# Convolution of the delta projections read from an SBUF copy with zero columns between the streams

## The chip, the cores and the metric

One core of a Trainium2 chip runs the whole program as one launch. The metric is the device time in microseconds (us) from its start to its end; the lower, the better. TensorE (PE) multiplies matrices into PSUM, VectorE (DVE), ScalarE (ACT) and GpSimd (POOL) work element by element, and SyncE (SP) issues most DMAs. Each engine runs its own instructions in the order in which they were queued, and waits on semaphores for the others.

## The reference

Two layers of a diffusion trunk over 256 context and 512 latent tokens of width 1024, in float32. Layer 0 mixes tokens by a gated delta rule, layer 1 by retention; each is followed by a squared-ReLU MLP. The change lies in layer 0, in the part between the projection and the recurrence:

```python
def short_conv(x, w):            # w: 4 taps for each channel, padding (2, 1)
    return lax.conv_general_dilated(x, w[:, None, :].astype(x.dtype), window_strides=(1,),
                                    padding=[CONV_PAD], dimension_numbers=('NWC', 'WIO', 'NWC'),
                                    feature_group_count=x.shape[-1])

def gdn_mixer(hc, hl, w_in, conv_w, ...):
    n_ctx = hc.shape[1]                                       # 256
    proj = jnp.concatenate([hc, hl], axis=1) @ w_in           # 768 tokens
    qkv = proj[..., :GDN_CONV_DIM]                            # 4096 channels: q 1024, k 1024, v 2048
    z = proj[..., GDN_CONV_DIM:GDN_CONV_DIM + GDN_VALUE_DIM]  # 2048 channels, no convolution
    qkv = jnp.concatenate([jax.nn.silu(short_conv(qkv[:, :n_ctx], conv_w)),
                           jax.nn.silu(short_conv(qkv[:, n_ctx:], conv_w))], axis=1)
    ...                          # l2norm of q and k, then chunks of 64 tokens, in both directions
```

The two streams, context and latent, are convolved apart: each begins and ends with zeros, and no tap reaches from one into the other.

## The kernel before, in words

Tokens lie on the free axis and channels on the 128 partitions. The projection is made in tiles of 128 channels: 32 convolution tiles (8 of q, 8 of k, 16 of v) and 16 z tiles. For one tile, w_cols loads the weights in two halves and splits each into a high and a low part (hl, one ACT and one DVE operation each; lines 55 to 57), and gemm_pair makes 24 matmuls of 512 latent columns into a PSUM tile gl and 24 of 256 context columns into gc. In this layer `self.gc = ("gl", 2)`, so gl and gc take turns in one ring of two PSUM slots: the gl of the next tile takes the slot of this tile's gl.

conv_tile then makes the four taps. ACT copies a segment from PSUM to acc, scaled by tap 2, and DVE adds taps 0, 1 and 3, each read from PSUM with its offset: three operations for gl (510 or 511 columns) and three for gc (254 or 255). The Silu of acc goes to kq (gdn_s1, k and q) or vt (gdn_sv, v). acc has two buffers in the pool prep, shared with sq, the squares for the norm, and with zs, the Silu of a z tile on its way to DRAM (z_tile).

Two heads make a pair, and there are eight. gdn_s1 and gdn_sv prepare the pair's k, q and v; gdn_bt makes decay factors e, 24 blocks of 128 columns first by a Relu (line 649), then by an Exp (657); gdn_s2 makes qkd and the triangular blocks, and eliminates in u (a select on POOL at 709, then 30 steps of two short DVE operations, 717 and 720); gdn_iv puts the inverse together (tt) through v32, xdg, pc and pc2; gdn_step runs twelve recurrence steps, each a chain from PE (kk, uo) through DVE (r, s) and ACT (und, un) back to PE; gdn_y normalises. layer0_mix issues the work of the next pairs between the steps of the present one, with priorities (PRI, P2, PS) for the steps and their preparation; convolution and z tiles fill the rest. A list scheduler turns this into the order of each queue, by the priorities and by when it takes operands and buffers to be ready; the order is fixed when the program is built. mod_rows (line 232) is further filling work. After the layer follow out0, the first MLP, the retention layer and the second MLP, which the change does not touch.

Of the kernel before, what the change touches and what calls it, by code (L numbers as in the profile page):

```python
# [10 lines left out]
F32 = mybir.dt.float32  # L11
BF16 = mybir.dt.bfloat16
F32R = mybir.dt.float32r
AF = mybir.ActivationFunctionType
ALU = mybir.AluOpType
# [4 lines left out]
NC_T = 256  # L20
NL_T = 512
T = NC_T + NL_T
# [3 lines left out]
NCH = 6  # L26
CH = 128
# [15 lines left out]
class Trunk:  # L43
# [393 lines left out]
    def z_tile(self, h, prep):  # L437
        nc = self.nc
        w = self.w_cols(self.i["gdn_w_in"][0][:, 4096 + h * 128:4096 + (h + 1) * 128])
        zs = prep.tile([128, T], F32, tag="acc", name="zs", bufs=2)  # L440
        for ps, t0, n in self.gemm_pair(w):
            nc.scalar.activation(out=zs[:, t0:t0 + n], in_=ps, func=AF.Silu)  # L442
        nc.sync.dma_start(out=self.zd[h], in_=zs)
# [128 lines left out]
    def conv_tile(self, prep, tile_i):  # L572
        nc = self.nc
        w = self.w_cols(self.i["gdn_w_in"][0][:, tile_i * 128:(tile_i + 1) * 128])
        c = [self.cw[:, j * 32 + tile_i:j * 32 + tile_i + 1] for j in range(4)]
        segs = self.gemm_pair(w)
        acc = prep.tile([128, T], F32, tag="acc", name="acc", bufs=2)
        for ps, t0, n in segs:
            nc.scalar.activation(out=acc[:, t0:t0 + n], in_=ps, func=AF.Copy, scale=c[2])  # L579
            for j, a, b in ((0, 2, 0), (1, 1, 0), (3, 0, 1)):  # L580
                m = n - max(a, b)
                nc.vector.scalar_tensor_tensor(  # L582
                    out=acc[:, t0 + a:t0 + a + m], in0=ps[:, b:b + m], scalar=c[j], in1=acc[:, t0 + a:t0 + a + m],
                    op0=ALU.mult, op1=ALU.add)
        return acc

    def gdn_s1(self, p, st, psk, scan, prep):
        nc = self.nc
        kq = scan.tile([128, NCH, 2 * CH], F32, tag="kq", name="kq", bufs=3)
        st["kq"] = kq  # L590
        acc = self.conv_tile(prep, 8 + p).rearrange("p (c i) -> p c i", i=CH)
        nc.scalar.activation(out=kq[:, :, 0:CH], in_=acc, func=AF.Silu)
        yield
        acc = self.conv_tile(prep, p).rearrange("p (c i) -> p c i", i=CH)
        nc.scalar.activation(out=kq[:, :, CH:2 * CH], in_=acc, func=AF.Silu)
        yield
        ps = psk.tile([128, 2, NCH], F32, tag="py", name="ssps")
        for hf in range(2):
            sq = prep.tile([128, 3, 2, CH], F32, tag="acc", name="sq", bufs=2)
            nc.scalar.activation(  # L600
                out=sq.rearrange("p c a i -> p c (a i)"), in_=kq[:, hf * 3:hf * 3 + 3], func=AF.Square)
            for c in range(3):
                for a in range(2):
                    nc.tensor.matmul(
                        ps[:, a, hf * 3 + c:hf * 3 + c + 1], lhsT=sq[:, c, a], rhs=self.ones[:, 0:1],
                        start=True, stop=True)
        ssk = prep.tile([128, NCH], F32, tag="ssk", name="ssk", bufs=2)
        sg = scan.tile([128, NCH], F32, tag="sg", name="sg", bufs=3)
        nc.vector.tensor_scalar_add(ssk, ps[:, 0], EPS)
        nc.vector.tensor_scalar(  # L610
            out=sg, in0=ps[:, 1], scalar1=128.0 * EPS, scalar2=EPS + 128.0 * EPS * EPS, op0=ALU.mult, op1=ALU.add)
        rk = prep.tile([128, NCH], F32, tag="rk", name="rk")
        self.rsq(rk, ssk)
        nk = scan.tile([128, NCH], F32, tag="nk", name="nk", bufs=3)
        nc.vector.scalar_tensor_tensor(out=nk, in0=ssk, scalar=-1.0, in1=rk, op0=ALU.mult, op1=ALU.mult)
        nc.gpsimd.tensor_tensor(out=rk, in0=rk, in1=rk, op=ALU.mult)
        we = scan.tile([128, 2, 2, NCH], F32, tag="we", name="we", bufs=3)
        for d in range(2):
            nc.gpsimd.tensor_tensor(
                out=we[:, d], in0=self.egl[:, d, 2 * p:2 * p + 2], in1=rk.unsqueeze(1).to_broadcast([128, 2, NCH]),  # L620
                op=ALU.mult)
        st.update(sg=sg, nk=nk, we=we, ssk=ssk)

    def gdn_sv(self, p, st, prep):
        vt = prep.tile([128, 2, T], F32, tag="vt", name="vt")
        st["vt"] = vt
        for h in range(2):
            acc = self.conv_tile(prep, 16 + 2 * p + h)
            self.nc.scalar.activation(out=vt[:, h], in_=acc, func=AF.Silu)
            yield  # L630

    def gdn_bt(self, p, st, prep):
# [92 lines left out]
    def gdn_iv(self, p, st, psk, prep, tags=("pp",), gate=None):  # L725
        nc = self.nc
        tts, vd, v64 = st["tts"], self.vd[p % 2], self.v64
        off32, off64 = st["off32"], st["off64"]
        N = 2 * NCH
        gsl = [slice(g * 32, (g + 1) * 32) for g in range(4)]  # L730
        half = [slice(0, 64), slice(64, 128)]
        with self.tc.issue_after(gate) if gate is not None else ExitStack():
            for d in range(2):
                nc.scalar.dma_start(
                    out=vd[d].rearrange("c g r q -> (c g) (r q)"), in_=self.u[d * 64:d * 64 + 48])
# [15 lines left out]
        ps = psk.tile([128, N, 32], F32, tag=next(tags), name="ivps")  # L751
# [14 lines left out]
        ps = psk.tile([128, N, 32], F32, tag=next(tags), name="ivps2")  # L766
# [8 lines left out]
            else:  # L775
                nc.vector.tensor_copy(dst, ps[gsl[ra]])
        yield
        pc2 = prep.tile([128, N, 64], F32, tag="pc2", name="pc2")
        for hf in range(2):
            cs = range(hf * NCH, (hf + 1) * NCH)  # L780
            ps = psk.tile([128, NCH, 64], F32, tag=next(tags), name="ivps4")
            for c in cs:
                for d in range(2):
                    nc.tensor.matmul(
                        ps[half[1 - d], c - hf * NCH], lhsT=off64[half[d], c], rhs=v64[half[d], c],
                        start=True, stop=True)
            if hf:
                nc.vector.tensor_copy(pc2[:, hf * NCH:(hf + 1) * NCH], ps)
            else:
                nc.scalar.activation(out=pc2[:, hf * NCH:(hf + 1) * NCH], in_=ps, func=AF.Copy)  # L790
        yield
        for hf in range(2):
            cs = range(hf * NCH, (hf + 1) * NCH)
            ps = psk.tile([128, NCH, 64], F32, tag=next(tags), name="ivps5")
            for c in cs:
                for d in range(2):
                    nc.tensor.matmul(
                        ps[half[d], c - hf * NCH], lhsT=pc2[half[1 - d], c], rhs=tts[d][half[1 - d], c, half[1 - d]],
                        start=True, stop=True)
            for d in range(2):  # L800
                dst = tts[d][half[d], hf * NCH:(hf + 1) * NCH, half[1 - d]]
                if d == 0:
                    nc.scalar.activation(out=dst, in_=ps[half[d]], func=AF.Copy)
                else:
                    nc.vector.tensor_copy(dst, ps[half[d]])
# [572 lines left out]
```

## Time and profile before

| | us |
|---|---|
| median of 3 runs | 2560.19 (2559.29 to 2561.56) |
| the profiled execution | 2564.44 |
| its span in the trace | 2562.7 |
| PE, DVE, ACT, POOL busy over the span | 2431.7, 1661.7, 1074.0, 163.7 |
| the stage of the convolutions, 60 to 890 us: PE, DVE, ACT, POOL busy | 735.59, 611.95, 486.93, 119.34 |

The profiled execution is a run of its own, 4.25 us above the median; durations and waits come from it alone. A row of the groups names the line, the engine and the operation, what it writes and reads, the shapes, the count, the busy time, the mean time of one in ns, and the idle time of the engine just before, with what ended it. A row of the waits says which engine and line waited for which, the total, how often, and the longest. A row in order of time has the start, the length, and in brackets the idle time ahead and its releaser. A row of the stretches has busy time and (instructions) of PE, weight loads, DVE, ACT and POOL, then the granted TensorE clock, the DMA share and GB/s.

### The profile page before, as it was taken

To read this page: it belongs to the slowest core of one execution; us is meant where nothing else is said; L and a number is where in the kernel's file an instruction comes from. 1 tells how busy PE (TensorE), PEld (TensorE's weight loads), DVE (VectorE), ACT (ScalarE), POOL (GpSimd) and SP (SyncE) were. 2 spreads that over 40 slices of the span, in tenths; PEclk is the share of its full clock that TensorE was granted. 3 is DMA by queue.
4 is the path that set the end of the run, shared out by engine and by line. 5 is a ranking of instruction groups with operands and counts; after the bars stand their busy time and mean duration, and the time that the engine had idled before them with its cause. 6 is when DMAs were issued, how large, how long until landed. Compare 5 with 4: busy or idle time off the path is not lost.

```text
span 2562.7 us, 38997 instructions
## 1 busy us (share of the span) xinstructions
PE 2431.7 (95%) x14879; PEld 2010.7 (78%) x14879; DVE 1661.7 (65%) x3382; ACT 1074.0 (42%) x2357; POOL 163.7 (6%) x248
## 2 busy tenths in 40 slices
PE   8799798998888999999999999999999999999998
PEld 4687686786777787878888888888888887788887
DVE  5568767777776845887876667874353546644446
ACT  5576556565654553253222222653231322532222
POOL 1101111111201110000000000000000000000000
PEclk9899899899999999999999999999999999999999
DMA  6332324333132238354444444243122223433332
GB/s 211 89 96 77 106 51 113 80 105 94 43 109 67 74 113 272 132 165 132 132 144 129 123 130 129 100 135 93 50 84 61 78 66 115 150 97 91 107 91 91
DMA packets 346828, 276.94 MB, mean 108 GB/s; under 512 B 105608, under 2 KB 293488, under 8 KB 346640
## 3 DMA queue, kind: packets, MB, share of 16 engines
q1 hardware_dynamic: 345616, 271.30, 35.2%
q10 hardware_dynamic: 1024, 3.15, 0.5%
q8 instruction: 117, 1.92, 0.3%
q14 instruction: 71, 0.58, 0.1%
HBM read 241.72 MB, written 32.67 MB: 107 GB/s over the span
## 4 chain that ended last, share of the span: by engine, by line
PE 58%; DVE 5%; DMA 2%; ACT 2%; issue 1%; POOL 0%; SPq 0%; POOLq 0%; DVEq 0%; ACTq 0%
PE pn L940 22%; PE gl L91 14%; PE rvp L1257 5%; PE gc L91 3%; PE rl L91 3%; PE rgp L1257 3%; PE pv L1287 3%; PE sc L1265 1%; PE rc L91 1%; PE nps L276 1%; DVE hl L57 0%; DVE ma L199 0%; DMA zt<-zd 0%; PE mps L214 0%; PE uo L865 0%
## 5 line engine op out<-in xcount | busy, mean ns | idle before, releaser
L91 PE MATMUL gl<-xt,hl 128*128 128x512 f32 (+2 forms) x2760 | 704.6, 404 | 53.9 <-DVE acc L582 31.9
L91 PEld LDWEIGHTS gl<-xt,hl 128*128 128x128 f32 x2760 | 517.0, 194 | 161.9 <-issue 27.9
L57 DVE TENSOR_TENSOR hl<-raw,hl 128x1024 fp32r<-128x1024 f32 (+1 forms) x306 | 321.4, 1052 | 231.1 <-ACT hl L56 230.3
L56 ACT ACTIVATE hl<-raw 128x1024 fp32r<-128x1024 f32 (+1 forms) x306 | 280.0, 920 | 409.6 <-PE pn L940 251.9
L940 PE MATMUL pn<-hl,fh 128*128 128x512 f32 x1920 | 444.7, 391 | 2.2 <-DVE fh L1074 1.9
L940 PEld LDWEIGHTS pn<-hl,fh 128*128 128x128 f32 x1920 | 357.3, 188 | 80.0 <-DVE fh L1074 5.0
L91 PE MATMUL gc<-xt,hl 128*128 128x256 f32 x1944 | 273.2, 289 | 8.9 <-DVE acc L582 4.7
L91 PEld LDWEIGHTS gc<-xt,hl 128*128 128x128 f32 x1944 | 253.3, 193 | 19.9 <-ACT zs L442 5.5
L199 DVE SCALAR_TENSOR_TENSOR ma<-mraw,cst,ma 128x256 f32<-128x256 f32 x280 | 123.5, 482 | 40.4 <-DMA mraw<-in_w_mod 38.1
L940 PE MATMUL pn<-hl,yh 128*128 128x512 f32 x576 | 133.8, 392 | 2.5 <-ACT yh L56 1.4
L954 DVE TENSOR_TENSOR facc<-pn,facc 128x512 f32<-128x512 f32 x120 | 82.5, 689 | 81.8 <-PE pn L940 81.5
L1257 PE MATMUL rvp<-hl,xt 128*128 128x512 f32 x576 | 132.8, 389 | 0.0
L940 PEld LDWEIGHTS pn<-hl,yh 128*128 128x128 f32 x576 | 107.2, 188 | 26.8 <-ACT yh L56 2.6
L1257 PEld LDWEIGHTS rvp<-hl,xt 128*128 128x128 f32 x576 | 107.8, 188 | 22.2
L1071 ACT ACTIVATE fr<-gl 128x512 f32<-128x512 f32 x64 | 38.2, 597 | 193.3 <-PE gl L91 190.7
L582 DVE SCALAR_TENSOR_TENSOR acc<-gl,cw,acc 128x511 f32<-128x511 f32 (+1 forms) x96 | 71.6, 746 | 37.9 <-ACT acc L579 37.1
L940 PE MATMUL pn<-hl,ryt 128*128 128x512 f32 x384 | 92.0, 397 | 0.0
L1257 PE MATMUL rgp<-hl,xt 128*128 128x512 f32 x384 | 91.0, 393 | 0.0
L91 PE MATMUL rl<-xt,hl 128*128 128x512 f32 x384 | 89.5, 391 | 0.4 <-DVE hl L57 0.4
L717 DVE TENSOR_TENSOR tmp<-u 112x30 f32<-112x30 f32 (+14 forms) x240 | 81.5, 339 | 9.4 <-POOL u L709 6.2
L940 PEld LDWEIGHTS pn<-hl,ryt 128*128 128x128 f32 x384 | 71.6, 188 | 16.8
L91 PEld LDWEIGHTS rl<-xt,hl 128*128 128x128 f32 x384 | 71.5, 188 | 15.7 <-DVE hl L57 0.9
(282 smaller groups left out, 3347.9 us busy)
## 6 DMA issues: line engine op xcount, KB each, us to landing
raw<-in_w_ff SPq DMA_DIRECT2D x128, 512.0 KB
mraw<-in_w_mod SPq DMA_DIRECT2D x112, 256.0 KB
raw<-in_gdn_w_in SPq DMA_DIRECT2D x96, 256.0 KB
raw<-in_ret_w_in SPq DMA_DIRECT2D x32, 512.0 KB
mraw<-in_w_mod SPq DMA_DIRECT2D x24, 512.0 KB
e<-gd SPq DMA_DIRECT2D x32, 384.0 KB
mraw<-in_w_mod SPq DMA_DIRECT2D x8, 1024.0 KB
raw<-in_gdn_w_out SPq DMA_DIRECT2D x16, 512.0 KB
```

What stands on the lines that cost most here:

```text
L56: nc.scalar.activation(out=hi, in_=src, func=AF.Copy)
L57: nc.vector.tensor_tensor(out=lo, in0=src, in1=hi.bitcast(F32), op=ALU.subtract)
L91: nc.tensor.matmul(ps, lhsT=w(a, k), rhs=xt[:, b, k, t0:t0 + n], start=(k == 0 and i == 0), stop=(k == 7 and i == 2))
L199: eng.scalar_tensor_tensor(out=accs[v], in0=raw[:, k], scalar=c, in1=accs[v], op0=ALU.mult, op1=ALU.add)
L276: nc.tensor.transpose(ps[:, k, :], xn[:, (half * 4 + k) * 128:(half * 4 + k + 1) * 128], self.ident)
L582: nc.vector.scalar_tensor_tensor(out=acc[:, t0 + a:t0 + a + m], in0=ps[:, b:b + m], scalar=c[j], in1=acc[:, t0 + a:t0 + a + m], op0=ALU.mu ...
L717: nc.vector.tensor_tensor(out=t3, in0=u3[:, 0:c, c:c + 1].to_broadcast([112, c, n]), in1=u3[:, c:c + 1, c + 1:32].to_broadcast([112, c, n] ...
L940: m = nc.tensor.matmul(ps, lhsT=lhs(a, k, t), rhs=hls[hf][k // 2][:, b, k % 2], start=(k == 0 and n == 0), stop=(k == 3 and n == 2))
L954: nc.vector.tensor_tensor(out=dst, in0=ps, in1=dst, op=ALU.add)
L1071: nc.scalar.activation(out=r, in_=ps, func=AF.Relu)
L1257: nc.tensor.matmul(ps, lhsT=xt[:, a, kk, t * 128:(t + 1) * 128], rhs=hls[kk // 2][:, b, kk % 2], start=(kk == 0 and n == 0), stop=(kk == 7 ...
L1287: nc.tensor.matmul(pvs[it], lhsT=pts[jt][:, i, it * 128:(it + 1) * 128], rhs=v[:, j, jt], start=(jt == 0 and n == 0), stop=(jt == 5 and n ...
```

## The change

Each convolution tile gets an SBUF tile xr of 773 columns: two zero columns, the 256 of the context, two zero columns, the 512 of the latent stream, one zero column. POOL writes the zeros in three memsets for each tile; ACT copies gc and gl from PSUM into their places without a scale. Then ACT makes acc, now 770 columns wide with the two between the streams, as tap 2 of xr, and DVE adds taps 0, 1 and 3 over all 770 columns at once, from xr. The Silu leaves out the middle columns and so comes in two pieces. acc (with sq) has one buffer instead of two; xr has two, and zs shares them. pc2 becomes two halves in the ring b32, which btt, v32, xdg and pc use already.

```diff
     def z_tile(self, h, prep):
...
-        zs = prep.tile([128, T], F32, tag="acc", name="zs", bufs=2)
+        zs = prep.tile([128, T], F32, tag="xr", name="zs", bufs=2)
...
         segs = self.gemm_pair(w)
-        acc = prep.tile([128, T], F32, tag="acc", name="acc", bufs=2)
+        xr = prep.tile([128, T + 5], F32, tag="xr", name="xr", bufs=2)
+        nc.gpsimd.memset(xr[:, 0:2], 0.0)
+        nc.gpsimd.memset(xr[:, NC_T + 2:NC_T + 4], 0.0)
+        nc.gpsimd.memset(xr[:, T + 4:T + 5], 0.0)
         for ps, t0, n in segs:
-            nc.scalar.activation(out=acc[:, t0:t0 + n], in_=ps, func=AF.Copy, scale=c[2])
-            for j, a, b in ((0, 2, 0), (1, 1, 0), (3, 0, 1)):
-                m = n - max(a, b)
-                nc.vector.scalar_tensor_tensor(
-                    out=acc[:, t0 + a:t0 + a + m], in0=ps[:, b:b + m], scalar=c[j], in1=acc[:, t0 + a:t0 + a + m],
-                    op0=ALU.mult, op1=ALU.add)
-        return acc
+            o = t0 + (4 if t0 else 2)
+            nc.scalar.activation(out=xr[:, o:o + n], in_=ps, func=AF.Copy)
+        acc = prep.tile([128, T + 2], F32, tag="acc", name="acc")
+        nc.scalar.activation(out=acc, in_=xr[:, 2:T + 4], func=AF.Copy, scale=c[2])
+        for j in (0, 1, 3):
+            nc.vector.scalar_tensor_tensor(
+                out=acc, in0=xr[:, j:j + T + 2], scalar=c[j], in1=acc, op0=ALU.mult, op1=ALU.add)
+        return ((0, 2, acc[:, 0:NC_T]), (2, 6, acc[:, NC_T + 2:T + 2]))
...
-        acc = self.conv_tile(prep, 8 + p).rearrange("p (c i) -> p c i", i=CH)
-        nc.scalar.activation(out=kq[:, :, 0:CH], in_=acc, func=AF.Silu)
+        for a, b, t in self.conv_tile(prep, 8 + p):
+            nc.scalar.activation(
+                out=kq[:, a:b, 0:CH], in_=t.rearrange("p (c i) -> p c i", i=CH), func=AF.Silu)
...
-            sq = prep.tile([128, 3, 2, CH], F32, tag="acc", name="sq", bufs=2)
+            sq = prep.tile([128, 3, 2, CH], F32, tag="acc", name="sq")
...
-            acc = self.conv_tile(prep, 16 + 2 * p + h)
-            self.nc.scalar.activation(out=vt[:, h], in_=acc, func=AF.Silu)
+            for a, b, t in self.conv_tile(prep, 16 + 2 * p + h):
+                self.nc.scalar.activation(out=vt[:, h, a * CH:b * CH], in_=t, func=AF.Silu)
...
-        pc2 = prep.tile([128, N, 64], F32, tag="pc2", name="pc2")
+        pc2 = [
+            prep.tile([128, N, 32], F32, tag="b32", name="pc2", bufs=2).rearrange("p (c a) i -> p c (a i)", a=2)
+            for _ in range(2)]
```

The scheduler puts the queues into a new order. In the fences that follow a row has the line (of the kernel in question), the operation, what it writes and reads with the tiles' numbers, and the shape.

ACT at about 380 to 397 us in the trace of before, where the Exp blocks of a pair's e0 and e1 run (L657 before, L663 after). Before:

```order
L56 ACTIVATE hl_3914<-raw_3912 128x512
L579 ACTIVATE acc_3569<-gc_3544,cw_429 128x256
L638 ACT_TABLE_LOAD
L638 ACTIVATE lk_4019<-ssk_3855 128x6
L56 ACTIVATE hl_4079<-raw_4077 128x512
L657 ACT_TABLE_LOAD
L657 ACTIVATE e0_4023<-e0_4023,lw_4018 128x128 x12
L657 ACTIVATE e1_4038<-e1_4038,lw_4018 128x128 x12
L629 ACT_TABLE_LOAD
L629 ACTIVATE vt_3508<-acc_3569 128x768
L579 ACTIVATE acc_3967<-gl_3917,cw_429 128x512
L579 ACTIVATE acc_3967<-gc_3942,cw_429 128x256
```

After, at the same place of the program (L583 is the copy to xr, L585 the scaled copy to acc):

```order
L56 ACTIVATE hl_4468<-raw_4466 128x512
L644 ACT_TABLE_LOAD
L644 ACTIVATE lk_4064<-ssk_3897 128x6
L583 ACTIVATE xr_4009<-gc_3984 128x256
L663 ACT_TABLE_LOAD
L663 ACTIVATE e0_4068<-e0_4068,lw_4063 128x128 x12
L663 ACTIVATE e1_4083<-e1_4083,lw_4063 128x128 x12
L56 ACTIVATE hl_4473<-raw_4471 128x512
L56 ACTIVATE hl_4641<-raw_4639 128x512
L585 ACTIVATE acc_4015<-xr_4009,cw_429 128x770
L442 ACT_TABLE_LOAD
L442 ACTIVATE zs_4132<-gl_4133 128x512
```

Before, the copies of the second v tile (acc_3967) stood behind the 24 Exp; now its gl and gc are copied ahead of them, and the copies of a z tile stand behind.

DVE at about 117 to 129 us, the first v tile of pair 0 and the beginning of the next. Before:

```order
L582 SCALAR_TENSOR_TENSOR acc_1046<-gl_996,cw_429,acc_1046 128x510
L582 SCALAR_TENSOR_TENSOR acc_1046<-gl_996,cw_429,acc_1046 128x511
L57 TENSOR_TENSOR hl_1069<-raw_1067,hl_1069 128x512
L582 SCALAR_TENSOR_TENSOR acc_1046<-gl_996,cw_429,acc_1046 128x511
L582 SCALAR_TENSOR_TENSOR acc_1046<-gc_1021,cw_429,acc_1046 128x254
L57 TENSOR_TENSOR hl_1141<-raw_1139,hl_1141 128x512
L582 SCALAR_TENSOR_TENSOR acc_1046<-gc_1021,cw_429,acc_1046 128x255 x2
L582 SCALAR_TENSOR_TENSOR acc_1122<-gl_1072,cw_429,acc_1122 128x510
```

After (L587 is the tap; L723 and L726 are the elimination in u):

```order
L57 TENSOR_TENSOR hl_1153<-raw_1151,hl_1153 128x512
L587 SCALAR_TENSOR_TENSOR acc_1058<-xr_1052,cw_429,acc_1058 128x770 x3
L57 TENSOR_TENSOR hl_1158<-raw_1156,hl_1158 128x512
L587 SCALAR_TENSOR_TENSOR acc_1137<-xr_1131,cw_429,acc_1137 128x770
L723 TENSOR_TENSOR tmp_982<-u_606 112x30
L587 SCALAR_TENSOR_TENSOR acc_1137<-xr_1131,cw_429,acc_1137 128x770
L726 TENSOR_TENSOR u_606<-u_606,tmp_982 112x30
```

Six taps with weight splits between them became three in a row, and no tap reads gl or gc any more.

POOL at about 113 to 126 us, from the copies of e to the select of u. Before:

```order
L699 COPY off64_953<-e0_800 64x768
L702 COPY off32_952<-e0_800 32x384 x2
L699 COPY off64_953<-e1_815 64x768
L702 COPY off32_952<-e1_815 32x384 x2
L709 AFFINE_SELECT u_606<-u_606 112x1024
L711 MEMSET u_606 112x32
```

After:

```order
L705 COPY off64_959<-e1_821 64x768
L708 COPY off32_958<-e1_821 32x384 x2
L578 MEMSET xr_1211 128x2
L579 MEMSET xr_1211 128x2
L580 MEMSET xr_1211 128x1
L715 AFFINE_SELECT u_606<-u_606 112x1024
L717 MEMSET u_606 112x32
```

The zero columns of a later tile's xr now stand ahead of the select with which the elimination begins.

More of the change, by code (lines that the diff above doesn't have):

```diff
@@ L590, in gdn_s1 @@
         st["kq"] = kq
-        acc = self.conv_tile(prep, 8 + p).rearrange("p (c i) -> p c i", i=CH)
-        nc.scalar.activation(out=kq[:, :, 0:CH], in_=acc, func=AF.Silu)
+        for a, b, t in self.conv_tile(prep, 8 + p):
+            nc.scalar.activation(
+                out=kq[:, a:b, 0:CH], in_=t.rearrange("p (c i) -> p c i", i=CH), func=AF.Silu)
         yield
-        acc = self.conv_tile(prep, p).rearrange("p (c i) -> p c i", i=CH)
-        nc.scalar.activation(out=kq[:, :, CH:2 * CH], in_=acc, func=AF.Silu)
+        for a, b, t in self.conv_tile(prep, p):
+            nc.scalar.activation(
+                out=kq[:, a:b, CH:2 * CH], in_=t.rearrange("p (c i) -> p c i", i=CH), func=AF.Silu)
         yield
@@ L787, in gdn_iv @@
             if hf:
-                nc.vector.tensor_copy(pc2[:, hf * NCH:(hf + 1) * NCH], ps)
+                nc.vector.tensor_copy(pc2[hf], ps)
             else:
-                nc.scalar.activation(out=pc2[:, hf * NCH:(hf + 1) * NCH], in_=ps, func=AF.Copy)
+                nc.scalar.activation(out=pc2[hf], in_=ps, func=AF.Copy)
         yield
@@ L797, in gdn_iv @@
                     nc.tensor.matmul(
-                        ps[half[d], c - hf * NCH], lhsT=pc2[half[1 - d], c], rhs=tts[d][half[1 - d], c, half[1 - d]],
+                        ps[half[d], c - hf * NCH], lhsT=pc2[hf][half[1 - d], c - hf * NCH], rhs=tts[d][half[1 - d], c, half[1 - d]],
                         start=True, stop=True)
```

## The prediction

> **What bounds the kernel now.** I read the page's first two parts, then the waits of TensorE in the stage that the change touches, then that stage in order of time, and last the durations by shape.
>
> ```profile
> PE 2431.7 (95%) x14879; PEld 2010.7 (78%) x14879; DVE 1661.7 (65%) x3382; ACT 1074.0 (42%) x2357; POOL 163.7 (6%) x248
> PE   8799798998888999999999999999999999999998
> 60.00:890.00 830.00, 735.59 (x6637) 612.93 (x6638) 611.95 (x1564) 486.93 (x1315) 119.34 (x174) 0.95 0.32 86
> ```
>
> Over the whole span PE is busy 95%, but the second row shows where it is not: the first fifteen slices, the delta layer, are the only ones below nine tenths. The third row is that stage, 60 to 890 us, which holds every convolution: PE busy 735.6 of 830 us, DVE 612 (74%), ACT 487 (59%), POOL 119 (14%), granted clock 0.95. So PE stands still for 94 us there, and the question is who ends these gaps. The waits of TensorE from 60 to 970 us, each with its total, count and longest:
>
> ```profile
> PE gl L91 <- DVE acc L582: 31.9, 11, 9.1
> PE yps L921 <- DVE o L915: 6.7, 8, 1.5
> PE ivps L754 <- DVE v L745: 6.3, 3, 5.9
> PE gl L91 <- ACT zs L442: 5.4, 1, 5.4
> PE gl L91 <- ACT hl L56: 5.1, 3, 4.2
> PE gc L91 <- DVE acc L582: 4.7, 2, 4.2
> PE kk L875 <- ACT und L870: 4.3, 7, 1.4
> PE gc L91 <- ACT zs L442: 4.2, 3, 3.2
> ```
>
> The largest item by far is PE waiting for the taps of L582: 31.9 + 4.7 = 36.6 us, over 32 convolution tiles 1.14 us a tile. Why it waits is seen in order of time (start, length, engine, and the idle time before it with its releaser):
>
> ```profile
> 120.53 7.33 PE L91 MATMUL gl<-xt,hl 128*128 128x512 f32 x24 [2.20 <-DVE acc L582]
> 127.70 3.03 PE L91 MATMUL gc<-xt,hl 128*128 128x256 f32 x24
> 127.90 0.69 ACT L579 ACTIVATE acc<-gl,cw 128x512 f32<-128x512 f32 x1 [4.67 <-PE gl L91]
> 128.62 1.54 DVE L582 SCALAR_TENSOR_TENSOR acc<-gl,cw,acc 128x510 f32<-128x510 f32 x2 [6.33 <-ACT acc L579]
> 130.67 0.75 DVE L582 SCALAR_TENSOR_TENSOR acc<-gl,cw,acc 128x511 f32<-128x511 f32 x1
> 131.56 5.71 PE L91 MATMUL gl<-xt,hl 128*128 128x512 f32 x24 [0.83 <-DVE acc L582]
> ```
>
> In this layer gl and gc share one ring of two PSUM slots (gemm_pair with gc set to "gl"), so the next tile's gl overwrites the gl of the tile just done. The cover for emptying it is one gc block, 3.03 us. Emptying takes the ACT copy (0.69) and three taps on DVE, here until 131.42, 3.5 us after the copy began: 0.83 us are missing even where DVE does little else. Where DVE is filled with other work it is far worse:
>
> ```profile
> 386.89 7.13 ACT L657 ACTIVATE e<-e,lw 128x128 f32<-128x128 f32 x24
> 396.09 0.67 ACT L579 ACTIVATE acc<-gl,cw 128x512 f32<-128x512 f32 x1
> 400.84 0.75 DVE L582 SCALAR_TENSOR_TENSOR acc<-gl,cw,acc 128x511 f32<-128x511 f32 x1
> 401.73 4.91 PE L91 MATMUL gl<-xt,hl 128*128 128x512 f32 x14 [9.06 <-DVE acc L582]
> 816.47 5.72 PE L91 MATMUL gl<-xt,hl 128*128 128x512 f32 x14 [6.96 <-DVE acc L582]
> ```
>
> At 401 us the copy was late (396.09, behind a block of Exp on ACT that began at 386.89), and the taps took another 5 us after it.
>
> **The change part by part.** *The eviction.* After the change a PSUM slot is free as soon as ACT has copied it to xr; DVE never reads it. The kernel has tiles that are already emptied in just this way, by ACT alone out of the same ring: the sixteen z tiles. In the rows above they cost PE 5.4 + 4.2 = 9.6 us, 0.60 us a tile. At that price the 32 convolution tiles cost 19.2 us instead of 36.6, a gain of 17.4. The ends: a copy that is always in time (4.67 us of ACT idle stood before the one at 127.90) gains all 36.6; if ACT is as late as DVE was, 0. I take the z price, since late copies behind Exp remain: in the order of the new ACT queue the zs copies still stand behind such a block.
>
> *The clock.* Matmuls just after a wait run slower: 24 of them took 7.33 us after 2.20 us of waiting and 5.71 us after 0.83 us, 1.62 us apart; the 14 after 9.06 and 6.96 us took 4.91 and 5.72, where 14/24 of 5.71 would be 3.33. So a wait of more than about 2 us costs some 1.6 us more. The 13 waits average 2.8 us; I take eight of them as long, an estimate, and with half of the waiting gone four: 6 us (ends 0 and 13). The Trainium skill ("TensorE: Matmul & The Clock Gate", What's actually happening) has the clock halve only after an idle window of about 3.4 us; by that rule the 2.20 us wait should have cost nothing, which the 7.33 us block contradicts, and the sum would gain some 2 us here and not 6.
>
> *The taps on DVE.* The rows by shape:
>
> ```profile
> L582 DVE SCALAR_TENSOR_TENSOR acc<-gl,cw,acc 128x511 f32<-128x511 f32 x64 | 47.7, 745 | 0.5
> L582 DVE SCALAR_TENSOR_TENSOR acc<-gc,cw,acc 128x255 f32<-128x255 f32 x64 | 30.4, 475 | 0.4
> L272 DVE SCALAR_TENSOR_TENSOR njunk<-o0acc,nr,nsc x6: 1285/1285/1287, 1082.3 to 1115.4; 128x1024 f32<-128x1024 f32 x6
> L199 DVE SCALAR_TENSOR_TENSOR ma<-mraw,cst,ma 128x256 f32<-128x256 f32 x280 | 123.5, 482 | 40.4 <-DMA mraw<-in_w_mod 38.1
> ```
>
> Six taps cost 3 x (745 + 475) = 3.66 us. The same operation wholly from SBUF takes 482 ns at 256 columns and 1285 at 1024, 1.046 ns a column, so 1.02 us at 770: three cost 3.06. DVE saves 0.60 us a tile, 19 us in all. At 74% busy I book none of it as time: PE's other waits for DVE (yps, ivps) come from the latency of short operations in the recurrence, and a 1.02 us tap in front of one of them holds it longer than one of 0.75. Ends: 6 us either way, about the 13 us of these two waits, halved.
>
> *ACT.*
>
> ```profile
> L579 ACT ACTIVATE acc<-gl,cw 128x512 f32<-128x512 f32 x32 | 22.0, 688 | 52.3 <-PE gl L91 52.1
> L579 ACT ACTIVATE acc<-gc,cw 128x256 f32<-128x256 f32 x32 | 15.3, 478 | 9.9 <-PE gc L91 9.8
> L629 ACT ACTIVATE vt<-acc 128x768 f32<-128x768 f32 x16 | 13.6, 848 | 31.9 <-DVE acc L582 31.9
> L952 ACT ACTIVATE facc<-pn x20: 597/598/601, 1150.9 to 2248.0; 128x512 f32<-128x512 f32 x20
> L442 ACT ACTIVATE zs<-gc x16: 362/384/417, 108.1 to 967.9; 128x256 f32<-128x256 f32 x16
> L1072 ACT ACTIVATE fh<-fr 128x512 fp32r<-128x512 f32 x64 | 40.1, 626 | 1.0
> L1072 ACT ACTIVATE fh<-fr 128x256 fp32r<-128x256 f32 x32 | 13.0, 407 | 0.1
> ```
>
> Before, a tile costs ACT 688 + 478 + 848 = 2.01 us. After: two plain copies 598 + 384, the scaled copy of 770 columns between 848 (768 columns without a scale) and 940 (with the 90 ns that a scale column adds: 688 against 598), and a Silu in two pieces, 626 + 407. With 940 that is 2.96 us, 0.95 more, 30 us over 32 tiles; ACT goes from 59% to 62% of the stage. PE's wait for ACT in the recurrence (und, 4.3 us) is what this touches; I book 2 us lost (ends 0 and 8).
>
> *The single acc slot.* acc and sq now have one buffer. The copy into acc waits for the Silu of the tile before, which stands ahead of it on ACT anyway; the second sq waits for six ssps matmuls of the first. That wait existed 6 times for 9.3 us (row below) and now comes 8 times: 3 us of ACT idle, behind which evictions queue, covered by the gc block. Booked at 0.
>
> ```profile
> ACT sq L600 <- PE ssps L604: 9.3, 6, 2.6
> POOL u L709 <- DMA u<-ud: 50.9, 8, 7.2
> L711 POOL MEMSET u<- 112x32 f32 x8 | 1.3, 158 | 0.5
> L860 POOL TENSOR_TENSOR o<-o,qs x48: 721/728/1665, 201.3 to 938.9; 128x256 f32<-128x256 f32 x48
> ```
>
> *The zero columns.* 96 memsets of a few columns on POOL, at most 158 ns each: 15 us on an engine that is busy 119 of 830. They wait for the old reader of the slot and hold what is queued behind; the select of u often stands right behind one, but waits 50.9 / 8 = 6.4 us for its DMA, which covers them. 0, and if that cover is gone 0.5 us on eight pairs, 4 us.
>
> *Taps and POOL.* POOL's sum of o takes 0.72 us and once 1.67, so something holds it at times. The Trainium skill ("SBUF — State Buffer", Who interferes with whom) says that a DVE instruction with two SBUF inputs and a GpSimd instruction that reads SBUF block each other wholly; the old taps had one SBUF input, the new ones two. An estimate by it: 96 taps of 1.02 us fill 12% of the stage, so about 21 of POOL's 174 operations there meet one and lose half a tap, 0.5 us, on average; if all 10 us reached PE, the sum would be 11 us of gain instead of 21. No row before shows this for the taps.
>
> *pc2* becomes two halves in the b32 ring, with the same copies; the slots' earlier readers (the transposes of xdg, the matmuls on pc) are done before the second-stage matmuls start: 0. *z tiles* move to the xr ring, still two buffers that wait for their store: 0. No load is added or moved by hand.
>
> *Sum:* -17.4 - 6 + 2 = -21 us. The profiled execution took 2564.4 us (span 2562.7), 4.2 above the median of 2560.2; its own time would be 2543, and the median 2539.
>
> **The rivals.** *All of the wait goes.* 36.6 us and the clock of eight long waits, 13: 2511. For it: the one at 127.90 us: the copy alone, at 598 ns, would have ended 2.2 us before the gc block did. Against it: the z tiles, which wait 0.60 us each under the same rule.
>
> *The wait changes its owner.* Copies come behind Exp and Silu on ACT as late as taps did, and what is saved is paid back: within 5 us of 2560. For it: the copy at 396.09 was late by ACT alone; PE waited from 392.67, so 4.0 us of those 9.06 would have stayed.
>
> *Slower: ACT stuck behind the taps.* In the new ACT order the next tile's gl copy stands a few rows behind the Silu of the tile before in 11 of 31 cases, and that Silu waits for the taps. The chain is scaled copy 0.94, taps, Silu 1.03, copy 0.60; the cover is a gl and a gc block, 5.71 + 3.03 = 8.74. With taps of 3.06 us it ends 3.1 us early. But the rows of DVE at 590 us show six taps stretched by other work:
>
> ```profile
> 590.29 0.75 DVE L582 SCALAR_TENSOR_TENSOR acc<-gl,cw,acc 128x510 f32<-128x510 f32 x1
> 600.97 0.47 DVE L582 SCALAR_TENSOR_TENSOR acc<-gc,cw,acc 128x255 f32<-128x255 f32 x1
> ```
>
> That is 11.15 us from first to last. Stretched so, the chain takes 13.7 us, 5.0 past its cover; on 11 tiles 55 us against the 36.6 saved, with 2 us for ACT: 2580. It decides from 9.5 us of taps on (36.6 / 11 = 3.3 past the cover). Against it: half as many taps offer half as many places to be pushed aside.
>
> **How the numbers follow.** The forecast, half of the wait gone, has 0.48 (its own range 2524 to 2552); all gone 0.18; the wait handed to ACT 0.13; slower 0.21, with which I also count an order of the queues that turns out worse by some other place. No change is within 0.2%, 5 us, about what a measurement of this kernel can tell. So faster 0.66, same 0.13, slower 0.21. The range 2508 to 2570 takes in the deep case and half of the slower one.
>
> **What would show it.** Right: no wait of PE on a tap; PE waiting for the xr copies some 19 us; taps near 1.02 us, 96 of them; ACT up by 30 us and DVE down by 19; PE's idle time from 60 to 890 us smaller by about 17, and the end of the delta layer earlier by about 21 with all later stages unchanged. Wrong: waits of PE on xr copies of 30 us or more; Silu waiting far longer than the 31.9 us that vt shows; the recurrence (und, r, s) waiting more; POOL operations or taps well above their old lengths.

## The result and the profile after

| | before | after |
|---|---|---|
| median, us | 2559.74 (2558.84 to 2561.56) | 2596.23 (2595.50 to 2597.70) |
| span of the profiled execution | 2562.7 | 2596.0 |
| PE's idle time over that span | 131.0 | 148.3 |
| PE's busy time over that span | 2431.7 | 2447.7 |

The changed kernel is slower: ratio 1.014 [1.0124, 1.0155]. The forecast was 2539, the range ended at 2570. The first rows of the page, the row of the taps, and the stretch from 60 to 890 us, all of after:

```profile
PE 2447.7 (94%) x14879; PEld 2019.0 (78%) x14879; DVE 1651.3 (64%) x3286; ACT 1093.1 (42%) x2419; POOL 174.5 (7%) x344
PE   8799798899889997999999999999999999999998
L587 DVE SCALAR_TENSOR_TENSOR acc<-xr,cw,acc 128x770 f32<-128x770 f32 x96 | 98.2, 1023 | 12.9 <-ACT acc L585 11.4
```

```profile
60.00:890.00 830.00, 732.79 (x6308) 607.68 (x6308) 580.76 (x1417) 496.22 (x1359) 127.35 (x262) 0.93 0.31 83
```

In the same 830 us PE finished 6308 matmuls instead of 6637, at a granted clock of 0.93 instead of 0.95. The taps are as worked out, 96 of 1.02 us. The main waits of PE from 60 to 1010 us:

```profile
PE knps L824 <- DVE mrow L236: 17.5, 4, 7.9
PE pn L948 <- ACT hl L56: 13.6, 1, 13.6
PE gl L91 <- ACT zs L442: 12.4, 2, 8.9
PE gl L91 <- DVE hl L57: 12.0, 4, 8.9
PE mps L232 <- DVE mrow L236: 11.8, 2, 6.2
PE kk L883 <- ACT und L878: 6.1, 10, 1.9
PE gl L91 <- ACT hl L56: 5.0, 3, 2.2
PE gc L91 <- ACT xr L583: 2.6, 5, 1.3
PE gl L91 <- ACT xr L583: 1.2, 1, 1.2
```

The wait for which the change was forecast to be good, PE on the emptying of a convolution tile, is gone but for 2.6 + 1.2 = 3.8 us: 36.6 before, so 33 us are saved, twice the 17.4 of the forecast. In its place stands one that was 4.3 us before (two rows of that trace, below): PE waits 17.5 + 11.8 = 29.3 us for mrow (L236), the four additions on DVE that finish a piece of the mod rows. These sums use the PSUM tile py, which the transposes of kn, nv and y use too. Late weight splits (hl) grew as well, and the first weights of out0 came 13.6 us late, once, against 0.8 before. The rows of before:

```profile
PE mps L232 <- DVE mrow L236: 3.9, 1, 3.9
PE pn L940 <- ACT hl L56: 0.8, 1, 0.8
PE knps L816 <- DVE mrow L236: 0.4, 2, 0.2
```

By engine, PE's waits on DVE fell from 71.3 to 59.0 us, though 36.6 of them were the taps, and its waits on ACT rose from 26.8 to 51.4. One place where PE waits for mrow in order of time, first DVE (L587 are taps, L723 and L726 steps of the elimination), then PE:

```profile
649.05 1.02 DVE L587 SCALAR_TENSOR_TENSOR acc<-xr,cw,acc 128x770 f32<-128x770 f32 x1
649.98 0.36 DVE L723 TENSOR_TENSOR tmp<-u 112x198 f32<-112x198 f32 x1
650.26 1.02 DVE L587 SCALAR_TENSOR_TENSOR acc<-xr,cw,acc 128x770 f32<-128x770 f32 x1
651.19 0.36 DVE L726 TENSOR_TENSOR u<-u,tmp 112x198 f32<-112x198 f32 x1
651.47 1.02 DVE L587 SCALAR_TENSOR_TENSOR acc<-xr,cw,acc 128x770 f32<-128x770 f32 x1
652.40 0.38 DVE L723 TENSOR_TENSOR tmp<-u 112x210 f32<-112x210 f32 x1
652.80 0.28 DVE L236 TENSOR_TENSOR mrow<-mps,mrow 2x128 f32<-2x128 f32 x1
...
654.62 0.29 DVE L236 TENSOR_TENSOR mrow<-mps,mrow 2x128 f32<-2x128 f32 x1
```

```profile
641.15 0.39 PE L232 MATMUL mps<-mraw,cst 128*2 128x128 f32 x6
645.68 1.35 PE L91 MATMUL gc<-xt,hl 128*128 128x256 f32 x10
654.97 0.69 PE L824 MATMUL knps<-ident,kq 128*128 128x128 f32 x2 [7.94 <-DVE mrow L236]
```

PE made the sums at 641 us. Their additions came on DVE from 652.80 on, behind taps of the next tile and elimination steps, and PE, whose next row was knps, stood still for 7.94 us.

*Where the 33.3 us between the two spans lie.* Idle time of PE up to the last y of the layer: 96.0 before, 99.3 after, so +3 in all (taps and copies -33, mrow +25, the rest weights, z and mraw). The late weights of out0: 13.6 instead of 0.8, +13. Busy time: +16 for the same 14879 matmuls. The trace's record of the granted clock has stretches at full and stretches at half clock; those at half clock add up to 105.0 us before and 146.0 after, and PE was busy for 74.1 and 96.5 us of them. If half of that is lost, an estimate, the clock accounts for 11 of the 16. The last y comes at 979 us instead of 946, so 34 later where the prediction looked for 21 earlier.

### The profile page after: what moved, and what is told of

Read it like the earlier page. It is cut to its first block, busy times and chain, and to the rows that moved or that the text cites. A ratio compares the mean times of both kernels' runs of the same rounds, so it can differ in the third digit from the quotient of the medians.

```text
span 2596.0 us, 39079 instructions
## 1 busy us (share of the span) xinstructions
PE 2447.7 (94%) x14879; PEld 2019.0 (78%) x14879; DVE 1651.3 (64%) x3286; ACT 1093.1 (42%) x2419; POOL 174.5 (7%) x344
## 4 chain that ended last, share of the span: by engine, by line
PE 78%; DVE 11%; ACT 5%; DMA 3%; issue 2%; POOL 1%; SPq 0%; POOLq 0%; ACTq 0%; DVEq 0%
PE pn L948 22%; PE gl L91 20%; PE gc L91 6%; PE rvp L1265 5%; PE rl L91 3%; PE rgp L1265 3%; PE pv L1295 2%; PE uo L873 1%; DVE acc L587 1%; PE sc L1273 1%; PE kk L883 1%; PE uo L894 1%; PE kk L855 1%; PE kk L856 1%; ACT e L663 1%
## 5 line engine op out<-in xcount | busy, mean ns | idle before, releaser
L91 PEld LDWEIGHTS gl<-xt,hl 128*128 128x128 f32 x2760 | 511.5, 192 | 142.3 <-DVE hl L57 14.4
L948 PE MATMUL pn<-hl,yh 128*128 128x512 f32 x576 | 135.5, 395 | 16.2 <-ACT hl L56 13.6
L948 PEld LDWEIGHTS pn<-hl,yh 128*128 128x128 f32 x576 | 108.3, 190 | 41.1 <-ACT hl L56 13.8
L587 DVE SCALAR_TENSOR_TENSOR acc<-xr,cw,acc 128x770 f32<-128x770 f32 x96 | 98.2, 1023 | 12.9 <-ACT acc L585 11.4
L723 DVE TENSOR_TENSOR tmp<-u 112x30 f32<-112x30 f32 (+14 forms) x240 | 79.8, 333 | 11.6 <-POOL u L715 8.4
L726 DVE TENSOR_TENSOR u<-u,tmp 112x30 f32<-112x30 f32 (+14 forms) x240 | 81.5, 340 | 3.6
```

The costliest lines, as they stand in the source:

```text
L91: nc.tensor.matmul(ps, lhsT=w(a, k), rhs=xt[:, b, k, t0:t0 + n], start=(k == 0 and i == 0), stop=(k == 7 and i == 2))
L587: nc.vector.scalar_tensor_tensor(out=acc, in0=xr[:, j:j + T + 2], scalar=c[j], in1=acc, op0=ALU.mult, op1=ALU.add)
L723: nc.vector.tensor_tensor(out=t3, in0=u3[:, 0:c, c:c + 1].to_broadcast([112, c, n]), in1=u3[:, c:c + 1, c + 1:32].to_broadcast([112, c, n] ...
L726: nc.vector.tensor_tensor(out=u3[:, 0:c, c + 1:32], in0=u3[:, 0:c, c + 1:32], in1=t3, op=ALU.subtract)
L948: m = nc.tensor.matmul(ps, lhsT=lhs(a, k, t), rhs=hls[hf][k // 2][:, b, k % 2], start=(k == 0 and n == 0), stop=(k == 3 and n == 2))
```

## The experiments

Each had the kernel before measured beside it on the same chip, at 2558 to 2562. Four theories of the loss stood first: A, the 96 small memsets on POOL; B, a worse order of the queues, with the mod rows late; C, the single slot of acc and sq; D, the wide taps.

**e1_persist**: two xr tiles that live through the stage, zeroed once, used in turn; z tiles use them too.

```diff
-        xr = prep.tile([128, T + 5], F32, tag="xr", name="xr", bufs=2)
-        nc.gpsimd.memset(xr[:, 0:2], 0.0)
-        nc.gpsimd.memset(xr[:, NC_T + 2:NC_T + 4], 0.0)
-        nc.gpsimd.memset(xr[:, T + 4:T + 5], 0.0)
+        xr = self.next_xr()
```

> The changed kernel, but the two xr tiles are allocated once and zeroed once, so that the 96 memsets of the stage are gone; z tiles write into the same two tiles and are stored in two pieces. Theory A (memsets on POOL wait for the slot's old reader and hold the select of u, the sums of o and the powers behind them): most of the 36 us come back, 2560 to 2575. Theory B (the new order of the queues, in which short DVE work such as the four mrow additions stands late behind taps): little comes back, 2585 to 2605, and the PE waits for mrow stay above 15 us. Theory C (the single acc slot): no change, 2590 to 2600. Theory D (wide taps): no change.

2584.79, ratio 1.0099 [1.0078, 1.012]: 11 us of 36 back. PE waited 32.6 us on mrow, more than after. A, C and D missed; B, whose range began at 2585, came nearest.

**e2_narrow**: eviction copies into a 768-wide xr without zero columns, six taps of the old widths from it, one Silu; acc single, pc2 in halves.

> Eviction alone: gl and gc are copied to an xr of 768 columns without zero columns, acc is made from it, the six narrow taps of before read xr instead of PSUM, one Silu; single acc, z tiles in the xr ring and pc2 in halves as in the changed kernel; no memsets. Theory A (memsets): 2535 to 2565, faster than or like before. Theory D (a tap of 1.02 us cannot be broken off, and short work waits behind it): 2540 to 2565 likewise. Theory C (single acc slot and ACT's longer queue): 2585 to 2605, like the changed kernel. Theory B (order): anywhere from 2550 to 2610, with another set of waits than the changed kernel.

2579.43, ratio 1.0084 [1.0062, 1.0106]. With narrow taps and no memsets 17 us came back; the wait on copies was 3.1 us, on mrow 11.4, on weight splits 50. A, C and D missed again, and only B's wide range holds it.

**e3_rings**: the old convolution from PSUM, with the new rings only: acc and sq one buffer, zs two of its own, pc2 in halves.

> The convolution of before (PSUM taps, six narrow), but acc with one buffer, z tiles in a ring of their own with two, pc2 in halves of the b32 ring. Theory C (the single acc slot is the cost): 2580 to 2610. Theories A and D: within 10 us of 2560. Theory B (order): moves by 5 to 25 us either way.

2591.85, ratio 1.0132 [1.0108, 1.0156]: 34 us lost against the kernel before beside it (2557.98), without any change to the convolution. That spoke for C and against A and D; B, with 25 us at most, missed. But its trace shows no wait of that size: PE waits 36.9 us on taps as before, 6.0 on mrow; its busy time is 2449.5, 18 us more than before.

The parts of e3 followed, one by one, and a control in which only a priority is changed. Theory R: pc2's halves are at fault; theory O: any new order of the queues costs or gains some 20 us by itself.

**e4_pc2**: before, with pc2 in halves.

> The kernel before with one edit: pc2 in two halves of the ring b32, the memory it frees left unused; convolution, acc, sq and zs as before. Theory R (the halves of pc2 tie the inverse of one pair to the block transposes of the next through a ring of two, and the queues are put in a worse order by it): most of the 34 us that all the ring changes cost together, so 2578 to 2595. Theory C (the single slot of acc and sq is what costs): 2553 to 2565, as before. Theory O (the work itself is not dearer; any edit that makes the scheduler place the queues anew loses 15 to 35 us, since the order before is an unusually good one): 2570 to 2595 too, so this run alone parts R and O from C.

2566.63, ratio 1.0026 [1.0016, 1.0036]: 7 us. R and O, which asked for 2570 at the least, both missed; C's range ended 2 us below.

**e5_acc1**: before, with `bufs=2` taken from acc and sq, and one buffer for zs.

> The kernel before with one edit: acc and sq share one buffer, zs has one buffer of its own; convolution from PSUM and pc2 as before. Theory C: 2575 to 2595, since the copy out of PSUM into acc now waits for the Silu of the tile before. Theory R: 2553 to 2565. Theory O: 2570 to 2595.

2563.18, ratio 1.0017 [1.0005, 1.0029]. C and O missed here. The parts cost 7 and 3 us, the whole 34: they don't add up, and R and C fall as causes. (zs has one buffer here and two in e3, so the two parts are not quite the whole.)

**e6_before_ps**: `PS = 200` instead of 250, in before.

> The kernel before with the priority PS of the preparation 200 instead of 250: the same instructions, tiles and buffers, in another order of the queues. Theory O: 2570 to 2595, a loss of the size of the change's although no work is changed. Theories R and C: 2553 to 2565, within a few us of before.

2578.95, ratio 1.0076 [1.0061, 1.0091]. Matmuls and the operations of DVE and POOL are the same in number, ACT loads a table once more, and 19 us are lost. O was the only theory that said so.

**e7_pc2own**: after, with pc2 in its own tile and one buffer for xr and zs.

```diff
-        zs = prep.tile([128, T], F32, tag="xr", name="zs", bufs=2)
+        zs = prep.tile([128, T], F32, tag="xr", name="zs")
...
-        xr = prep.tile([128, T + 5], F32, tag="xr", name="xr", bufs=2)
+        xr = prep.tile([128, T + 5], F32, tag="xr", name="xr")
...
-        pc2 = [
-            prep.tile([128, N, 32], F32, tag="b32", name="pc2", bufs=2).rearrange("p (c a) i -> p c (a i)", a=2)
-            for _ in range(2)]
+        pc2 = prep.tile([128, N, 64], F32, tag="pc2", name="pc2")
```

> The changed kernel with pc2 in a tile of its own again; the memory comes from xr (shared with zs), which has one buffer. Convolution from xr with wide taps, one acc. Theory R: the loss goes, 2535 to 2560, although the eviction copy now waits for the taps of the tile before. Theory C: the loss stays or grows, 2590 to 2620, since xr and acc are both single. Theory O: 2565 to 2605, anywhere.

2546.57, ratio 0.9946 [0.9926, 0.9967]: faster than both kernels. R's range holds it, O's began at 2565 and missed. Which of its two edits did it, and would it stay under another priority?

**e8_after_ps**: after, with `PS = 200`.

> The changed kernel with PS 200 instead of 250, the edit that cost the kernel before 19 us. Theory O (the order drawn by the scheduler decides, within some 20 us either way): 2560 to 2610, and no reason for it to stay at 2596. Theory R (the memory plan of the change, pc2 in b32 with two xr, is what costs): 2588 to 2604.

2573.24, ratio 1.0048 [1.0033, 1.0064]. The edit that cost before 19 us gives after 23; at this setting the change gains 6, though single runs of the two overlap (2571.8 to 2580.2, and 2577.4 to 2583.4). R is out.

**e9_pc2own_ps**: e7 with `PS = 200`.

> The version with pc2 in its own tile and one xr (2546.6), with PS 200. Theory R: it stays fast, 2537 to 2558. Theory O: 2540 to 2590, most likely slower by 10 us or more, since a fast order is given up.

2564.34, ratio 1.0009 [0.9996, 1.0021]: most of e7's gain is gone. O's range holds it, R's does not.

**e10_xr1**: after, with one buffer for xr and zs, pc2 left in halves.

> The changed kernel with one buffer for xr and zs instead of two, pc2 left in its two halves. Theory X (two xr let the projections run ahead, which puts taps and mod rows in front of the recurrence): the loss goes, 2537 to 2560. Theory R (pc2's halves): the loss stays, 2585 to 2605. Theory O: anywhere from 2545 to 2605.

2549.65, ratio 0.9957 [0.994, 0.9973]. So pc2 has no part in e7's gain, and theory X looked right.

**e11_persist1**: e7 with one lasting xr and no memsets.

> The version with pc2 in its own tile, and one xr that lives through the stage: its zero columns are written once and the 96 memsets are gone; z tiles use it too and are stored in two DMAs. If the memsets and what they hold up cost what the earlier run without them gave back (11 us): 2530 to 2542. If that was another draw of the order: 2540 to 2575.

2595.72, ratio 1.0127 [1.0112, 1.0142]. Both ranges missed. Taking 96 memsets away cost 49 us here and gave 11 in e1. A steady cost of the memsets does not fit both; the two versions also differ in their order.

**e12_before_pri, e13_after_pri, e14_xr1_pri**: `PRI = 350` instead of 300 in before, after and e10. Theory M: the late mod rows are a steady cost of the change.

> The kernel before with the priority PRI of the recurrence steps 350 instead of 300: same work, another order. Theory O (orders of one and the same work scatter by some 15 us, and the order of before is one of the better ones): 2562 to 2590. Theory M (what costs is in the change's own work: late additions of the mod rows): 2555 to 2566.

> The changed kernel with PRI 350. Theory O: 2550 to 2600, and against the kernel before with PRI 350 within 20 us either way. Theory M: slower than that one by 20 us or more, with mod rows again among the largest waits.

> The changed kernel with one buffer for xr and zs (2549.7), with PRI 350. Theory X (one xr is better in itself): 2540 to 2556, and below the other two of this setting. Theory O: 2545 to 2590, no better on average than the changed kernel.

2560.39, 2585.79 and 2594.54, ratios 0.9998 [0.9984, 1.0012], 1.0085 [1.0058, 1.0113] and 1.0122 [1.0105, 1.014]. M held in both of its ranges, for before and for after. O missed both: before by 2 us, and the 25 us between the two are more than its 20. X fell, and O's range for e14 ended 5 us below.

**e15_after_pp**: after, with the mod rows' sums in another PSUM tile.

```diff
-            self.mod_rows(prep, psk, "py", 0, ch, q) for ch in (2, 3, 4) for q in range(8)]
+            self.mod_rows(prep, psk, "pp", 0, ch, q) for ch in (2, 3, 4) for q in range(8)]
```

> The changed kernel with the sums of the mod rows in the PSUM tile pp instead of py, so that the transposes of kn, nv and y no longer wait for their four additions on DVE. Theory M (those additions, late behind taps, are the loss: 29 us of PE waiting): 2560 to 2575, and no wait of knps on mrow. Theory O: 2555 to 2605, the wait gone and its time possibly at another place.

2586.19, ratio 1.0083 [1.0054, 1.0112]. The largest waits of its PE:

```profile
PE pn L948 <- ACT hl L56: 12.4, 1, 12.4
PE nvps L830 <- ACT vt L635: 7.7, 2, 7.2
PE gl L91 <- ACT zs L442: 7.3, 1, 7.3
PE kk L855 <- DVE s L890: 5.5, 6, 2.6
PE kk L883 <- ACT und L878: 5.4, 9, 1.0
PE uo L873 <- DVE r L859: 5.3, 12, 0.9
```

mrow fell from 29.3 to 3.6 us, and 10 us of time came back, not the 21 to 36 that M asked for: PE now waits for DVE inside the recurrence (s, r) and for vt. The edit also gave the queues another order, so how much of the 10 us is mrow's is not shown.

**e16_before_g3, e17_after_g3, e18_xr1_g3**: `G3 = {11: 3}` in before, after and e10, a fourth order for before and after.

> The kernel before with G3 {11: 3} instead of {11: 4}: three instead of four pieces of the elimination of a later pair are issued behind the last step; same work, a fourth order. Theory O: 2558 to 2582. Theory M: 2555 to 2566.

> The changed kernel with G3 {11: 3}. Theory O: 2550 to 2600, within 20 us of the kernel before with the same G3, either way. Theory M (late additions of the mod rows cost 15 us or more in every order of this work): slower than that one by 12 us or more, PE waiting over 12 us on mrow.

> The changed kernel with one buffer for xr and zs, with G3 {11: 3}. Theory X (one xr is better in itself; the 2594.5 at PRI 350 was an accident): 2540 to 2556. Theory O: 2548 to 2596.

2583.17, 2584.56 and 2550.90, ratios 1.0083 [1.0062, 1.0104], 1.0096 [1.0075, 1.0117] and 0.9958 [0.9943, 0.9972]. Before, both theories missed, O by 1 us and M by 17. For after O held; M's wait on mrow came (37.6 us), its loss of 12 us did not. The edit left the queues of e10 as they were, so e18 measures that kernel once more and says nothing for X. The waits that matter, first of e16, then of e17:

```profile
PE gl L91 <- DVE acc L582: 21.9, 12, 4.1
PE gc L91 <- DVE acc L582: 19.2, 8, 3.8
PE mps L232 <- DVE mrow L236: 4.3, 1, 4.3
```

```profile
PE knps L824 <- DVE mrow L236: 24.0, 3, 9.7
PE mps L232 <- DVE mrow L236: 13.6, 3, 6.2
PE gl L91 <- ACT xr L583: 4.6, 2, 2.8
PE gc L91 <- ACT xr L583: 3.3, 6, 1.2
```

Put together, the change under four settings (medians; PE's waits on taps or copies, on mrow, and on weight splits, from 60 to 1010 us of each trace):

| setting | before | after | change | taps/copies | mrow | hl |
|---|---|---|---|---|---|---|
| as given | 2559.7 | 2596.2 | +36 | 36.6, 3.8 | 4.3, 29.3 | 12.3, 30.6 |
| PS 200 | 2579.0 | 2573.2 | -6 | 41.4, 5.0 | 8.0, 13.5 | 9.1, 20.6 |
| PRI 350 | 2560.4 | 2585.8 | +25 | 45.2, 6.7 | 3.2, 41.9 | 8.5, 16.1 |
| G3 {11: 3} | 2583.2 | 2584.6 | +1 | 41.1, 7.9 | 4.8, 37.6 | 6.6, 11.3 |
| mean | 2570.6 | 2584.9 | +14 | 41.1, 5.9 | 5.1, 30.6 | 9.1, 19.7 |

Two things are shown by it. The waits move the same way in all four orders; in the mean 35 us less on the eviction, 25.5 more on mod rows, 10.5 more on weights. PE's waiting has not shrunk, it has changed its owner: by engine its waits on DVE went from 75.8 to 62.2 us in the mean, those on ACT from 23.1 to 41.5. And the time scatters: one and the same work gave 2560 to 2583 before and 2573 to 2596 after. The mean of the four differences, 14 us, has a standard error of 10, so four orders don't tell it from zero.

How firmly an order fixes the time, three kernels show that differ in the text but not in the queues. In e7, e10 and e18 the five queues are the same row by row (line and tile numbers left out): 2546.6, 2549.7 and 2550.9, though single runs of e7 go from 2537 to 2556. No two of the other kernels have the same queue on PE.

## Why the prediction was wrong

*The eviction.* Right in kind and too small: no tap holds PE any more, and copies held it for 3.8 us where the price of the z tiles gave 19. ACT was in time; the z price, which came from waits behind blocks of e (Exp and Relu), was the wrong row to take, the 4.67 us of ACT idle at 127.90 the right one.

*The step that failed first* is "At 74% busy I book none of it as time", with its bound of 6 us. I listed as PE's other waits for DVE only yps and ivps. DVE is a queue that lags, and as long as PE met the lag at the taps, it met it nowhere else for long. Freed of the taps, it ran on to the next place where it needs DVE: the mod rows, in py. That wait stood in the trace before (3.9 us in one piece, L232 on L236) and in no part of the sum. PE waits 25 us more there, and 11 more for weight splits, in the mean of the orders; together 36 against 35 saved. The traces show the sums of it in four orders; that it is DVE's lag that moved is my reading of them. For it: as given, PE's waits on DVE fell by 12 us only, where 37 on taps were taken away, and in e15 PE met DVE in the recurrence once py was out of its way. As given, term by term: the eviction -33 us (booked -17.4), the mod rows +25 and the weight splits +18 (both in no term of the sum), the clock some +11 (booked -6), und +2 (booked 2). That is 23 of the 33 us between the spans; the other 10 are smaller waits and busy time that these terms don't explain.

*The rivals.* "The wait changes its owner" was nearest, at 0.13: right that all is paid back, wrong in the new owner and in the time. It expected late copies; they came to 3.8 us, and PE met mrow on DVE instead. Its waits on ACT did grow by 25 us, but at weight splits, z tiles and other places. "ACT stuck behind the taps" did not happen: vt waited 23.3 us for taps, less than the 31.9 before. I had put "an order of the queues that turns out worse by some other place" into the slower 0.21 without a size; this is what came. The range left it out: a scatter of 20 us either way about any forecast could have been read from no row of one trace.

*The clock.* Booked as -6, as a price for each long wait; the busy time came out 16 higher, some 11 of it at half clock. Waits above 2 us did fall, from 15 to 10, and yet the clock went down. So the number of long waits does not set it. The stretch from 60 to 890 us of e10 and of e15, which both have 8 such waits up to the last y:

```profile
60.00:890.00 830.00, 743.00 (x6860) 620.33 (x6859) 595.08 (x1479) 507.38 (x1397) 130.93 (x268) 0.96 0.33 88
```

```profile
60.00:890.00 830.00, 746.56 (x6379) 624.67 (x6378) 596.88 (x1442) 505.19 (x1375) 126.97 (x264) 0.93 0.31 83
```

By the rule in the Trainium skill ("TensorE: Matmul & The Clock Gate", What's actually happening), an idle window of about 3.4 us halves the clock; e15 has 3 waits above that and e10 7, and e15 has the lower clock.

The traces show more. In all 20 of them, from 60 to 1010 us, the half clock begins and ends on a grid of 3.41 us. Of the grid's steps at full clock, each of the 195 in which PE was busy for less than 40% was followed by a step at half clock; of those with 40 to 60% busy 63 of 170 were, and above 60% only 69 of 4566, for which the traces name no reason. The half clock ended only behind a step with at least 83% busy. Four steps of before, around the block of 7.33 us from which the prediction took its price:

```profile
114.76:118.17 3.41, 3.41 (x28) 3.25 (x26) 3.25 (x6) 1.32 (x2) 2.31 (x5) 1.00 0.60 95
118.17:121.59 3.42, 1.22 (x7) 0.92 (x6) 3.38 (x7) 0.99 (x2) 0.00 (x0) 1.00 0.50 111
121.59:125.00 3.41, 3.41 (x10) 2.67 (x9) 0.66 (x2) 0.84 (x1) 0.63 (x1) 0.50 0.87 271
125.00:128.41 3.41, 3.41 (x19) 2.92 (x18) 0.00 (x0) 0.51 (x1) 0.80 (x2) 1.00 0.04 17
```

The wait of 2.20 us left PE busy for 1.22 of the 3.42 us of one step, and the next one ran at half clock (0.50 in its row). So the price hangs on how much of a step is idle, and not on a wait's length alone; short waits that fall together can cost it too. What is lost then is lost while PE computes: it was busy at half clock for 105.1 us in e15 and for 44.7 in e10, whose long waits take up much of the slow stretches themselves.

*Terms that held.* Taps: 1.023 us against 1.02, all of them 98.2 us instead of 117.2, the 19 foreseen. ACT's rows: scaled copy 945 ns (940), plain copies 599 and 381 (598 and 384). The recurrence's wait on und: 6.1 instead of 4.3, +1.8 against the 2 booked. The wait of sq: 13.2 us in 8 pieces, 8 as foreseen. pc2: e7 and e10 have one order whichever way it is kept; in the kernel before its halves alone (e4) came with another order and 7 us.

*Zero columns.* Here the cover of the select was indeed gone at times. POOL in order of time at 435 us:

```profile
434.92 0.10 POOL L578 MEMSET xr<- 128x2 f32 x1 [12.13 <-DVE acc L587]
434.96 0.09 POOL L579 MEMSET xr<- 128x2 f32 x1
434.99 0.09 POOL L580 MEMSET xr<- 128x1 f32 x1
435.16 1.26 POOL L715 TENSOR_SCALAR_AFFINE_SELECT u<-u 112x1024 f32<-112x1024 f32 x1
```

The memset costs 0.1 us; the wait of 12.13 us for the slot's last reader, in front of a select, is what I had not priced. The select waited for its DMA 5 times, where it had been 8. Its share of the time is not shown: e1 and e11, both without it, gained 11 and lost 49.

*Taps and POOL.* The sums of o on POOL and the taps, each with minimum, median and maximum in ns, of after:

```profile
L868 POOL TENSOR_TENSOR o<-o,qs x48: 721/727/2579, 202.8 to 970.4; 128x256 f32<-128x256 f32 x48
L587 DVE SCALAR_TENSOR_TENSOR acc<-xr,cw,acc x96: 967/1016/1594, 71.7 to 902.2; 128x770 f32<-128x770 f32 x96
```

The median of o is where it was (728), the longest went from 1665 to 2579; over 48 sums the mean rose from 813 to 868 ns, 2.6 us in all. The block that the Trainium skill ("SBUF — State Buffer", Who interferes with whom) has between such a tap and POOL can be in the few long ones; the estimate of 10 us by it was too much.

*What beats both.* The change with one buffer for xr (e10, and e7 and e18 with the same queues) takes 2547 to 2551, 11 to 14 us less than before. The largest waits of e10:

```profile
PE gl L91 <- DVE hl L57: 41.8, 6, 7.5
PE gl L91 <- ACT zs L442: 10.0, 3, 8.9
PE yps L929 <- ACT qs L864: 6.7, 6, 1.2
```

mrow takes 0.6 us there. Against before, its span is 15.2 us shorter, and 13.8 of them are busy time (2417.9 instead of 2431.7) for the same matmuls: PE was busy at half clock for 44.7 us instead of 74.1. It is a good order and not a better design as far as shown: the same text with PRI 350 (e14) takes 2594.5, with zs 36.6 and mrow 14.8.

## What to carry to other kernels

Where a list scheduler orders the queues, as here, a change's time is the change plus a new draw of the order. Measure how far the time moves when only a priority is changed, before and after, and judge a change by several draws; a row of one trace prices only the work. When you take a wait off an engine that lags, look for the next place where the bound engine needs it, and put that wait into the sum as the gain's likely taker. Price a wait of PE with the clock that follows it: lay the trace out in steps of its clock record, and count those in which PE is busy for less than half.

## What the runs showed of the hardware that was not expected

The same 14879 matmuls kept PE busy from 2417.9 us (e10, mean clock 0.984) to 2453.5 (e15, 0.973). The product of the two is 2379 and 2387, and 2383 for before (0.980): most of the difference is the granted clock, worth up to 36 us in this kernel.

The clock was halved in steps of 3.41 us, and a step with PE busy for less than 40% was always followed by one at half clock (195 of 195 in 20 traces), also where no single wait was as long as a step, such as the 2.20 us in before. Over the 20 traces the time at half clock goes from 82.0 us (e10) to 153.4 (e11). Taking half of PE's busy time at half clock as lost, an estimate, this loss goes from 22 to 57 us and PE's idle time from 125 to 151, while the rest of the busy time stays within 2387 to 2401. So the scatter between the orders lies in PE's idle time and in this clock together.
